# x's second half loaded a step later and normalised by VectorE, and 44 products of constants ahead of the first modulation product

## The chip, the cores and the metric

The kernel runs on one core of one Trainium2 chip. A core has TensorE (PE in the rows; its weight load is PEld), VectorE (DVE), ScalarE (ACT), GpSimd (POOL) and SyncE (SP), which here issues most DMA transfers. The metric is the device time of one execution in microseconds (us); less is better.

## The reference

One layer of a diffusion backbone: 1024 tokens x 1024 channels, 256 context tokens, all in float32. What matters here is its beginning:

```python
shift, scale, gate = jnp.split(jax.nn.silu(c) @ w_mod[i] + b_mod[i], 3, axis=-1)
mod_c = jax.nn.silu(c_ctx) @ w_mod[i] + b_mod[i]
h = _layer_norm(x) * (1.0 + scale[:, None]) + shift[:, None]
hc = _layer_norm(ctx) * (1.0 + mod_c[D_MODEL:2 * D_MODEL]) + mod_c[:D_MODEL]
discs = [_discretise(ssm_lam_re[i, k], ssm_lam_im[i, k], ssm_log_dt[i, k],
                     ssm_b_re[i, k], ssm_b_im[i, k]) for k in range(2)]
u_ctx = hc @ w_in[i][:, :D_SSM] + b_in[i][:D_SSM]
...
ua, za, ub, vb, zb, ga, gb = _split_proj(h @ w_in[i] + b_in[i])
y_a, _ = _s5_bidir(ua, discs, ssm_c_re[i], ssm_c_im[i], ssm_d[i], ctx_final, True)
```

Behind it come the two branches (the bidirectional S5 scan `y_a`, and a spatial gating unit), their gates, an output projection and a LayerNorm of the residual. `_discretise` turns the S5 parameters into the scan's coefficients, elementwise on arrays of 64 x 64.

## The kernel before

Every product in float32 precision is made of three products of rounded halves (`mm3`, lines L82, L83, L84: high x high, low x high, high x low). So each operand is split into a high part, which ScalarE writes (a rounding copy), and a low part, which VectorE subtracts (`split`, L77 and L78).

The stage of the change is the first 90 us. Its work goes over eight blocks k of 128 input channels, and over two halves of the tokens: half 0 is the tiles x0 to x3, half 1 is x4 to x7 (each 128 tokens x 1024 channels, 512 KB). Per block:

- `load_wm(k)` loads two blocks of w_mod of 512 KB; they take buffers of a pool of six, so those of k + 3 wait for the products of k. `load_uw` loads a raw chunk of the weight of `ua` (for two k) and splits it.
- `mod_mm(k)` makes the modulation product `pm` (8 products, 16 records), `mod(k)` copies it on VectorE (`mrow`), brings it into columns with products `pmc` on TensorE and adds the bias on VectorE (`mods`).
- `trans_pe(k, hf)` transposes block k of four tiles of x on TensorE (`pt`); `trans_mod` reads it on ScalarE with scale and shift (`hf`), rounds it on ScalarE (`hh`) and takes the low part on VectorE (`hl`).
- `ua_step(k, hf)` runs the 12 products `pu` of the block, into four PSUM banks that collect over k.

`norm_rows` is LayerNorm without its gain: statistics on VectorE, a power -0.5 on GpSimd, a small operation on VectorE, and the normalisation itself on ScalarE (L198). Only x3 is normalised by VectorE (L453). The first loop runs the eight steps of half 0 and prepares block k + 2 within step k; in steps 1 to 4 it also loads and normalises x4 to x7. The second loop runs half 1 and the context tiles (`trans_c`: `pc`, `ch`, `cl`). The discretisation stands as a list `later` of small VectorE operations (tiles `disc`, then `cmul` with its scratch `cmu` and `cmv`, and the results `pw` and `pb`); `issue(n)` puts the next n of them into the order: 8 in each step of half 0, 12 in each of half 1. When `pb` is there, VectorE and GpSimd make the products `ab`. Behind the second loop TensorE goes on with `pcu`, the context's input projection. `ua_out` reads the banks of a half on ScalarE (`ut`).

A scheduler of the framework sets the final order of each engine from the order in the code and from its own estimates; `tc.issue_after(i)` holds the instructions in it back until behind instruction i. Each engine, and SP's queue of loads, then works strictly in its order.

Much later, at 405 to 436 us, `y_mm(b)` makes the scan's output for four blocks b from tables that `y_tables(b)` loads: `ca` for two directions, then `mt`.

Of the kernel before, what the change touches and what calls it, by code (L numbers as in the profile page):

```python
# [12 lines left out]
OP = mybir.AluOpType  # L13
# [23 lines left out]
def mixer_kernel(ctx: ExitStack, tc: tile.TileContext, a, out):  # L37
    nc = tc.nc
    V, S, Pl, PE = nc.vector, nc.scalar, nc.gpsimd, nc.tensor
# [5 lines left out]
    def pool_of(tag, bufs, dshape, ddt=F32):  # L45
        def make(name, shape=dshape, dt=ddt):
            return sb.tile(list(shape), dt, name=name, tag=tag, bufs=bufs)
        return make
# [5 lines left out]
    TMP = pool_of("tmp", 4, (128, 512))  # L54
    ROW = pool_of("row", 2, (128, 1280))
    ST = pool_of("st", 12, (128, 12))

    def C(name, shape, dt=F32):
        return sb.tile(list(shape), dt, name=name)

    def BANK(name, shape=(128, 512)):
        return psum.tile(list(shape), F32, name=name, tag="b", bufs=8)

    def dma(o, i):
        nc.sync.dma_start(o, i)

    def dma_side(o, i):

# [23 lines left out]
    def emit_load():  # L92
        key, ap, shape, eng = jobs[emitted[0]]
        emitted[0] += 1
        raw = RAW("r_" + key, shape)
        dma(raw, ap)
        hi, lo = WSP("h_" + key, shape), WSP("l_" + key, shape)
        split(hi, lo, raw, eng)
        loaded[key] = (hi, lo)
# [29 lines left out]

    cc = C("cc", [128, 8, 2])  # L130
    dma(cc, a["cc"])
    wmt = {}

    def load_wm(k):
        for s in range(2):
            wmt[k, s] = WSP(f"wm{k}{s}", (128, 4, 256), F32)
            dma(wmt[k, s], a["wm"][k, s])

    xv = a["x"].rearrange("(t p) d -> t p d", p=128)
    xn = {}  # L140

    def load_x(t):
        xn[t] = G(f"x{t}")
        dma(xn[t], xv[t])
# [15 lines left out]
    ident = C("ident", [128, 128])  # L160
# [3 lines left out]
    ones = C("ones", [128, 128])  # L164
# [15 lines left out]
    def moments(src, name):  # L180

        n = src.shape[-1] // 512
        st = ST(name + "s")[:, :6 * n].rearrange("p (n s) -> p n s", n=n)
        for i in range(n):
            V.bn_stats(st[:, i, :], src[:, i * 512:(i + 1) * 512])
        return finish(st, name)

    def finish(st, name):
        mv = ST(name + "m")
        V.bn_aggr(mv[:, 0:2], st)  # L190
        V.tensor_scalar(mv[:, 2:3], mv[:, 1:2], EPS, None, op0=OP.add)
        Pl.tensor_tensor(mv[:, 3:4], mv[:, 2:3], half, op=OP.pow)
        return mv, mv[:, 0:1], mv[:, 3:4]

    def norm_rows(x, name):
        mv, mu, rs = moments(x, name)
        V.scalar_tensor_tensor(mv[:, 4:5], mu, -1.0, rs, op0=OP.mult, op1=OP.mult)
        S.activation(x, x, AF.Identity, bias=mv[:, 4:5], scale=rs)  # L198
# [21 lines left out]
    def mod(k):  # L220
        if k not in pms:
            mod_mm(k)
        pm = pms[k]
        row = TMP("mrow")
        V.tensor_copy(row[:, 0:256], pm[:, 0:256])
        pc = BANK(f"pmc{k}")
        for s in range(2):
            PE.matmul(pc[:, 2 * s:2 * s + 2], row[:, 128 * s:128 * s + 128], fold[:, 0:2], start=True, stop=True)
        V.tensor_tensor(mods[:, k], pc[:, 0:4].rearrange("p (s n) -> p s n", s=2),
                        cols[:, k:k + 9:8].unsqueeze(2).to_broadcast([128, 2, 2]), op=OP.add)  # L230
# [3 lines left out]
    def trans_pe(k, hf):  # L234
        if hth[k] is None:
            hth[k] = G(f"hh{k}", dt=F32R)
            htl[k] = G(f"hl{k}", dt=F32R)
        p = pts[k, hf] = BANK(f"pt{k}{hf}")
        for i in range(4):
            PE.transpose(p[:, i * 128:(i + 1) * 128], xn[4 * hf + i][:, k * 128:(k + 1) * 128], ident)  # L240

    def trans_mod(k, hf):
        sl = slice(hf * 512, hf * 512 + 512)
        modulate(hth[k][:, sl], htl[k][:, sl], pts[k, hf], k, 0)

    def trans_h(k, hf):
        trans_pe(k, hf)
        trans_mod(k, hf)
# [4 lines left out]
    def load_uw(q):  # L253
        raw = RAW(f"uw{q}", (128, 2, 512))
        dma(raw, a["w_ua"][q])
        split(uw[:, 0, q], uw[:, 1, q], raw, V)
# [10 lines left out]
    def ua_step(k, hf):  # L267
        sl = slice(hf * 512, hf * 512 + 512)
        for b in range(4):
            if k == 0:  # L270
                acc[b] = BANK(f"pu{b}{hf}")
            mm3(acc[b], *uwk(k, b), hth[k][:, sl], htl[k][:, sl], k == 0, k == 7)
# [5 lines left out]
    def ua_out(hf):  # L278
        for b in range(4):
            if hf == 0:  # L280
                ut.append(WSP(f"ut{b}", (128, T, 128), F32))
            S.activation(ut[b][:, :, 64 * hf:64 * hf + 64], acc[b].rearrange("p (c t) -> p t c", t=T),
                         AF.Identity, bias=cols[:, C_UA + b:C_UA + b + 1])
            if hf == 1:
                dma(ud[b].rearrange("t p c -> p t c")[:, :, 32:160], ut[b])
# [8 lines left out]
    def issue(n):  # L294
        for f in later[:n]:
            f()
        del later[:n]
# [13 lines left out]
    def cp(o, x, scale=1.0):  # L311
        later.append(lambda: S.activation(o, x, AF.Copy, scale=scale))
# [34 lines left out]
    q, w, z, sn, cs, odd, eve, sg = (r_[i] for i in range(3, 11))  # L347
# [57 lines left out]
    def cmul(dst, x, yr, yi):  # L405

        n, w = x.shape[1], x.shape[3]

        def f():
            u = TMP("cmu", (128, 256 // w, 2, w))[:, :n]  # L410
            v = TMP("cmv", (128, 256 // w, 2, w))[:, :n]
            for o, y in ((u, yr), (v, yi)):
                V.tensor_tensor(o, x, y.unsqueeze(1).unsqueeze(1).to_broadcast([128, n, 2, w]), op=OP.mult)
            V.tensor_tensor(dst[:, :, 0, :], u[:, :, 0, :], v[:, :, 1, :], op=OP.subtract)
            V.tensor_tensor(dst[:, :, 1, :], u[:, :, 1, :], v[:, :, 0, :], op=OP.add)
        later.append(f)

    n = 1
# [27 lines left out]
    pc = pwf  # L446
    cp(pc[:, :, :, 0:32], pw[:, :, :, 0:32])

    with tc.issue_after(folded.ins):
        for t in range(3):  # L450
            norm_rows(xn[t], f"lx{t}")
        _, mu, rs = moments(xn[3], "lx3")
        normed = V.tensor_scalar(xn[3], xn[3], mu, rs, op0=OP.subtract, op1=OP.mult)  # L453

    with tc.issue_after(mod_mm(0).ins):
        trans_pe(0, 0)
# [8 lines left out]
    for k in range(8):  # L465
        if k >= 6:
            trans_h(k - 6, 1)
        ua_step(k, 0)
        if k >= 1 and k < 5:
            load_x(k + 3)  # L470
            norm_rows(xn[k + 3], f"lx{k + 3}")
        if k + 2 < 8:
            load_wm(k + 2)
            if k in (0, 1, 3):
                load_uw((k + 3) // 2)
            trans_pe(k + 2, 0)
            mod(k + 2)
            trans_mod(k + 2, 0)
        issue(8)

    xc = []
    for j in range(2):
        t = RAW(f"xc{j}")
# [5 lines left out]
    def trans_c(k):  # L489
        p = BANK(f"pc{k}")  # L490
        for j in range(2):
            PE.transpose(p[:, j * 128:(j + 1) * 128], xc[j][:, k * 128:(k + 1) * 128], ident)
        modulate(cth[k // 4][:, k % 4, :], ctl[k // 4][:, k % 4, :], p[:, :256], k, 1)
    ua_out(0)
    for k in range(8):
        if k + 2 < 8:
            trans_h(k + 2, 1)
        ua_step(k, 1)
        trans_c(k)
        issue(12)  # L500
    ua_out(1)

    weights("blk0", 0)
# [16 lines left out]
    for b in range(4):  # L520
        p = BANK(f"pcu{b}")
# [126 lines left out]
    mtd = dram.tile([4, 128, 8, 128], F32, name="mtd")  # L648

    cad = dram.tile([4, 2, 128, 1024], F32, name="cad")  # L650
# [67 lines left out]
    for q in range(4):  # L718
        wh, wl = weights(f"vb{q}")
        for kk in range(8):  # L720
            ks = slice(128 * kk, 128 * kk + 128)
            for j in range(2):
                k = 2 * q + j
# [4 lines left out]
    for kk in range(8):  # L728
        if kk % 2 == 0:
            vpair = G(f"vt{kk}", (128, 2, 512))  # L730
        v = vpair[:, kk % 2, :]
# [15 lines left out]
    for cb in range(4):  # L747
        V.scalar_tensor_tensor(sgb[:, cb, :], prs[:, cb, :], cols[:, C_LB + cb:C_LB + cb + 1], sgb[:, cb, :],
                               op0=OP.mult, op1=OP.add)
# [49 lines left out]
            then(t, p, sl)  # L799


    cas, mts, ums, zs, gks, gt = {}, {}, {}, {}, {}, []

    def y_tables(b):
        for d in range(2):
            ca = WSP(f"ca{b}{d}", (128, 8, 8, 16), F32)
            dma(ca.rearrange("p g i h -> p (g i h)"), cad[b, d])
            cas[b, d] = ca
        mts[b] = RAW(f"mt{b}", (128, 8, 128))
        dma(mts[b], mtd[b])  # L810
        if b < 2:
            y_rows(b)

    def y_rows(b):
        src = ud[b].rearrange("t (h g) c -> (t h) g c", g=8)[:, :, 32:160]
        if b < 2:
            t = ROW(f"um{b}", (128, 8, 128))
            dma(t, src)
            ums[b] = [t[:, g, :] for g in range(8)]
        else:  # L820
            ts_ = [TMP(f"um{b}{h}", (128, 4, 128)) for h in range(2)]
            for h, t in enumerate(ts_):
                dma(t, src[:, 4 * h:4 * h + 4])
            ums[b] = [ts_[g // 4][:, g % 4, :] for g in range(8)]
# [273 lines left out]
    for i in range(0, 8, 2):  # L1098
# [15 lines left out]
        if i == 0:  # L1114

            for h in range(2):
                p = BANK(f"pga{h}")
# [72 lines left out]
    for t in range(4, 8):  # L1190
        w = 512 if t < 7 else 256
# [67 lines left out]
```

## Time and profile before

| | us |
|---|---|
| time, median of 3 runs | 728.3 (727.65 to 730.11) |
| the profiled execution | 724.48 |
| its span, first to last instruction | 722.7 |
| TensorE busy | 692.4 (96% of the span) |
| VectorE busy | 528.4 (73%) |
| ScalarE busy | 252.5 (35%) |
| GpSimd busy | 92.0 (13%) |

The mean granted clock of TensorE was 0.994. Busy times are sums over the whole span; the stage of the change has a profile of its own, which is read from waits and timelines. In a timeline row stand the start, the busy time, engine, line, operation, output<-inputs, shape and count, and in brackets the idle time ahead of it with what ended it.

### The profile page before, as it was taken

The page shows a single profiled execution, that of the slowest core. Times are in us where ns is not written, and L with a number is a line of the kernel's source. Part 1 is how long each engine was busy: PE and PEld are TensorE (multiplying, and loading weights), DVE is VectorE, ACT ScalarE, POOL GpSimd, SP SyncE. Part 2 cuts the span into 40 slices and gives each one's busy share as a digit, 9 for nine tenths or more (in the row PEclk, how much of TensorE's full clock was granted, in tenths as well). Part 3 has the DMA queues.
Part 4 walks back from the last instruction along what each step waited for, and adds up shares of the span by engine and source line. Part 5 has one row for each costly group of instructions (what it writes and reads, how often), then busy time and mean ns, then how long its engine had stood idle before and what let it go on. Part 6 is the DMA issues. An engine that isn't in the chain of part 4 may idle for free.

```text
span 722.7 us, 10220 instructions
## 1 busy us (share of the span) xinstructions
PE 692.4 (96%) x3876; PEld 573.8 (79%) x3876; DVE 528.4 (73%) x1148; ACT 252.5 (35%) x364; POOL 92.0 (13%) x145
## 2 busy tenths in 40 slices
PE   3989999999999999999999999999999999999993
PEld 1657798888888888888888898888888878888883
DVE  5586954469889485898989399736678669953993
ACT  4348737652013523211112366324353522310000
POOL 1000134006642100000000000001111000000220
PEclk9999999999999999999999999999999999999997
DMA  7950283624721321121213753234557951251421
GB/s 304 412 194 2 58 219 125 183 79 169 230 77 34 107 70 56 58 88 59 88 59 94 250 210 102 88 106 171 173 188 284 411 214 40 88 175 57 176 88 59
DMA packets 41394, 101.96 MB, mean 141 GB/s; under 512 B 8961, under 2 KB 17793, under 8 KB 41345
## 3 DMA queue, kind: packets, MB, share of 16 engines
q1 hardware_dynamic: 35072, 84.04, 33.6%
q0 software_dynamic: 6272, 17.28, 7.0%
q8 instruction: 30, 0.49, 0.3%
q14 instruction: 20, 0.16, 0.1%
HBM read 79.31 MB, written 24.08 MB: 143 GB/s over the span
## 4 chain that ended last, share of the span: by engine, by line
PE 90%; DVE 3%; DMA 2%; ACT 2%; issue 1%; SPq 0%; POOL 0%; DVEq 0%
PE pp L82 10%; PE pp L83 10%; PE pp L84 10%; PE po L1155 4%; PE po L1154 4%; PE po L1153 4%; PE pb L84 4%; PE pb L83 4%; PE pb L82 4%; PE pg L83 4%; PE pg L82 4%; PE pg L84 4%; PE pv L572 3%; PE pvb L725 2%; PE pvb L724 2%; PE pvb L726 2%
## 5 line engine op out<-in xcount | busy, mean ns | idle before, releaser
L82 PE MATMUL pp<-hh,h_blk 128*128 128x512 f32 x320 | 125.3, 392 | 0.0
L83 PE MATMUL pp<-hh,l_blk 128*128 128x512 f32 x320 | 124.6, 389 | 0.0
L84 PE MATMUL pp<-hl,h_blk 128*128 128x512 f32 x320 | 124.5, 389 | 0.0
L82 PEld LDWEIGHTS pp<-hh,h_blk 128*128 128x128 f32 x320 | 60.1, 188 | 13.2 <-ACT vst L574 0.5
L84 PEld LDWEIGHTS pp<-hl,h_blk 128*128 128x128 f32 x320 | 60.1, 188 | 12.5
L83 PEld LDWEIGHTS pp<-hh,l_blk 128*128 128x128 f32 x320 | 60.1, 188 | 12.2
L634 DVE TENSOR_TENSOR scm<-acat,vst 128x128 f32<-128x128 f32 x158 | 46.0, 291 | 9.8 <-ACT vst L574 5.0
L77 ACT ACTIVATE h_blk<-r_blk 128x1024 fp32r<-128x1024 f32 x20 | 21.4, 1070 | 54.6 <-PE pp L83 21.7
L638 DVE TENSOR_TENSOR vst<-vst,scs 128x64 f32<-128x64 f32 x158 | 35.3, 224 | 4.9
L637 DVE TENSOR_TENSOR scs<-scm 128x64 f32<-128x64 f32 x158 | 35.4, 224 | 4.6
L78 DVE TENSOR_TENSOR l_blk<-r_blk,h_blk 128x1024 fp32r<-128x1024 f32 x20 | 25.2, 1258 | 17.0 <-ACT h_blk L77 17.0
L1153 PE MATMUL po<-wobig,mh 128*128 128x512 f32 (+1 forms) x90 | 32.9, 365 | 0.0
L1154 PE MATMUL po<-wobig,mh 128*128 128x512 f32 (+1 forms) x90 | 32.9, 365 | 0.0
L1155 PE MATMUL po<-wobig,ml 128*128 128x512 f32 (+1 forms) x90 | 32.9, 365 | 0.0
L82 PE MATMUL pu<-hh,uw 128*128 128x512 f32 x64 | 26.8, 419 | 3.9 <-ACT hh L208 3.9
L1165 DVE TENSOR_TENSOR r<-po,xr 128x512 f32<-128x512 f32 (+1 forms) x18 | 11.0, 618 | 22.2 <-PE po L1155 22.2
L788 ACT ACTIVATE act<-pp,cols 128x512 f32<-128x512 f32 x16 | 10.8, 678 | 46.5 <-issue 19.0
L84 PE MATMUL pu<-hl,uw 128*128 128x512 f32 x64 | 25.2, 406 | 1.1 <-DVE hl L209 1.1
L69 POOL DMA_DIRECT2D md<-mb x8 | 4.3, 543 | 168.1 <-DVE scs L637 110.7
L82 PE MATMUL pb<-yas,h_w_a 128*128 128x512 f32 x64 | 25.3, 395 | 0.0
L83 PE MATMUL pu<-hh,uw 128*128 128x512 f32 x64 | 25.3, 395 | 0.0
L725 PE MATMUL pvb<-l_vb,hh 128*128 128x512 f32 x64 | 25.0, 391 | 0.0
(415 smaller groups left out, 1711.7 us busy)
## 6 DMA issues: line engine op xcount, KB each, us to landing
r_blk<-in_w_blk SPq DMA_DIRECT2D x20, 512.0 KB, 3.4
wm<-in_wm SPq DMA_DIRECT2D x16, 512.0 KB, 8.2
x<-in_x SPq DMA_DIRECT2D x8, 512.0 KB, 6.8
cad<-kca POOLq DMA_DIRECT2D x8, 512.0 KB, 3.3
md<-mb POOLq DMA_DIRECT2D x8, 512.0 KB, 3.2
ca<-cad SPq DMA_DIRECT2D x8, 512.0 KB, 5.6
ga<-in_w_blk SPq DMA_DIRECT2D x8, 512.0 KB, 3.7
wgt<-in_w_gate SPq DMA_DIRECT2D x8, 512.0 KB, 3.6
```

The costliest lines, as they stand in the source:

```text
L78: return first, (eng or V).tensor_tensor(lo, src, hi.bitcast(F32), op=OP.subtract)
L82: PE.matmul(o, wh, rh, start=first, stop=False, skip_group_check=more)
L83: PE.matmul(o, wl, rh, start=False, stop=False, skip_group_check=more)
L84: PE.matmul(o, wh, rl, start=False, stop=last, skip_group_check=more)
L572: PE.matmul(p[64 * par:64 * par + 64, c, 0:160], abt[:, 2 * q + par, 64 * c:64 * c + 64], u160[b][:, 2 * q + par, :], start=True, stop=True)
L634: V.tensor_tensor(scm, acat.rearrange("p d (o c) q -> p d o (c q)", o=2), both(n - 1, prev).unsqueeze(2).to_broadcast([128, 2, 2, 32]), op ...
L637: V.tensor_tensor(scs4, m4[:, :, 0, :], m4[:, :, 1, :], op=OP.add)
L638: V.tensor_tensor(both(n, 160 if n == 31 else cur), both(n, cur), scs2, op=OP.add)
L725: PE.matmul(pvb[kk], hth[k][:, ks], wl[:, j, :], start=False, stop=False)
L1153: PE.matmul(p, mh, wh, start=k == 0, stop=False)
L1154: PE.matmul(p, mh, wl, start=False, stop=False)
L1155: PE.matmul(p, ml, wh, start=False, stop=k == 7)
```

## The change

Four things, in the diff below. 44 products of two constant tiles (`ones`, `ident`) stand at the head of the program for TensorE, into a bank that nobody reads. x4 to x7 are loaded behind the w_mod blocks of steps 2, 3 and 4 (the last two together) and normalised one step after that by VectorE, in place (`norm_here`). The list `later` is issued 8 at a time up to step 4, then 4, and 14 in the second loop; the scratch of `cmul` lies in the ROW buffers. In `y_tables` the table mt of block 3 is loaded behind the two `ca` of block 2.

```diff
 def dma(o, i):
-        nc.sync.dma_start(o, i)
+        return nc.sync.dma_start(o, i)
...
+    def norm_here(t):
+        _, mu, rs = moments(xn[t], f"lx{t}")
+        return V.tensor_scalar(xn[t], xn[t], mu, rs, op0=OP.subtract, op1=OP.mult)
...
-            u = TMP("cmu", (128, 256 // w, 2, w))[:, :n]
-            v = TMP("cmv", (128, 256 // w, 2, w))[:, :n]
+            u, v = (ROW(t)[:, 0:512].rearrange("p (n c w) -> p n c w", c=2, w=w)[:, :n] for t in ("cmu", "cmv"))
...
+    warm = BANK("warm")
+    for i in range(44):
+        PE.matmul(warm[:, 0:128], ones, ident, start=True, stop=True)
     with tc.issue_after(folded.ins):
         for t in range(3):
             norm_rows(xn[t], f"lx{t}")
-        _, mu, rs = moments(xn[3], "lx3")
-        normed = V.tensor_scalar(xn[3], xn[3], mu, rs, op0=OP.subtract, op1=OP.mult)
+        normed = norm_here(3)
...
         ua_step(k, 0)
-        if k >= 1 and k < 5:
-            load_x(k + 3)
-            norm_rows(xn[k + 3], f"lx{k + 3}")
         if k + 2 < 8:
             load_wm(k + 2)
+
+            for t in {2: (4,), 3: (5,), 4: (6, 7)}.get(k, ()):
+                load_x(t)
             if k in (0, 1, 3):
                 load_uw((k + 3) // 2)
             trans_pe(k + 2, 0)
             mod(k + 2)
             trans_mod(k + 2, 0)
-        issue(8)
+        for t in {3: (4,), 4: (5,), 5: (6, 7)}.get(k, ()):
+            norm_here(t)
+        issue(8 if k < 5 else 4)
...
         trans_c(k)
-        issue(12)
+        issue(14)
...
-            dma(ca.rearrange("p g i h -> p (g i h)"), cad[b, d])
+            ca_last[b] = dma(ca.rearrange("p g i h -> p (g i h)"), cad[b, d])
...
-        dma(mts[b], mtd[b])
+        if b == 3:
+
+            with tc.issue_after(ca_last[2].ins):
+                dma(mts[b], mtd[b])
+        else:
+            dma(mts[b], mtd[b])
```

How that moves the instructions, at three places. First SP's queue of loads, from x4 on. In the order before x_277, x_342, x_403 and x_468 are x4 to x7, wm_353 and wm_355 the blocks of k = 4, wm_414 and wm_416 those of k = 5, wm_479 and wm_481 of k = 6, uw_418 the chunk uw3:

```order
L65 DMA x_277<-in_x 128x1024
L65 DMA wm_353<-in_wm 128x1024
L65 DMA wm_355<-in_wm 128x1024
L65 DMA wm_414<-in_wm 128x1024
L65 DMA x_342<-in_x 128x1024
L65 DMA wm_416<-in_wm 128x1024
L65 DMA uw_418<-in_w_ua 128x1024
L65 DMA x_403<-in_x 128x1024
L65 DMA wm_479<-in_wm 128x1024
L65 DMA wm_481<-in_wm 128x1024
```

And after, where the blocks of k = 4 are wm_376 and wm_378, those of k = 5 wm_428 and wm_430, of k = 6 wm_492 and wm_494, and x_380 is x4:

```order
L65 DMA wm_376<-in_wm 128x1024
L65 DMA wm_378<-in_wm 128x1024
L65 DMA wm_428<-in_wm 128x1024
L65 DMA wm_430<-in_wm 128x1024
L65 DMA uw_434<-in_w_ua 128x1024
L65 DMA x_380<-in_x 128x1024
L65 DMA wm_492<-in_wm 128x1024
L65 DMA wm_494<-in_wm 128x1024
L65 DMA x_432<-in_x 128x1024
```

x4 now goes behind five loads that it stood ahead of; the loads in front of this place stand as they did.

Second, ScalarE from the split of uw0 on. Before (hh_160 is of k = 0, hh_179 of k = 1, hh_231 of k = 2, hh_296 of k = 3, hh_357 of k = 4; uw_227, uw_292 and uw_418 are the chunks uw1, uw2 and uw3):

```order
L77 ACTIVATE uw<-uw_79 128x512 x2
L207 ACTIVATE hf<-pt_162,mods 128x512
L208 ACTIVATE hh_160<-hf 128x512
L207 ACTIVATE hf<-pt_181,mods 128x512
L208 ACTIVATE hh_179<-hf 128x512
L77 ACTIVATE uw<-uw_227 128x1024
...
L198 ACTIVATE x_277<-x_277,lx4m 128x1024
L207 ACTIVATE hf<-pt_359,mods 128x512
L208 ACTIVATE hh_357<-hf 128x512
L198 ACTIVATE x_342<-x_342,lx5m 128x1024
L77 ACTIVATE uw<-uw_418 128x1024
L207 ACTIVATE hf<-pt_424,mods 128x512
```

After (hh_205 is of k = 0, hh_224 of k = 1, hh_276 of k = 2, hh_330 of k = 3; uw_272, uw_326 and uw_434 are uw1, uw2 and uw3):

```order
L77 ACTIVATE uw<-uw_79 128x512 x2
L211 ACTIVATE hf<-pt_207,mods 128x512
L212 ACTIVATE hh_205<-hf 128x512
L77 ACTIVATE uw<-uw_272 128x1024
L211 ACTIVATE hf<-pt_226,mods 128x512
L212 ACTIVATE hh_224<-hf 128x512
L77 ACTIVATE uw<-uw_326 128x1024
L211 ACTIVATE hf<-pt_278,mods 128x512
L212 ACTIVATE hh_276<-hf 128x512
L211 ACTIVATE hf<-pt_332,mods 128x512
L212 ACTIVATE hh_330<-hf 128x512
L77 ACTIVATE uw<-uw_434 128x1024
```

The normalisations of x4 to x7 are gone from this engine, and the split of uw1 has moved ahead of `hf` of k = 1.

Third, VectorE at the end of the second half. Before (hl_534 is the last `hl`, that of k = 7; cl_650 belongs to the context, ab_1089 is the first of the products `ab`):

```order
L413 TENSOR_TENSOR cmu<-pw,disc 128x448
L414 TENSOR_TENSOR pb<-cmu,cmv 128x7x32
L415 TENSOR_TENSOR pb<-cmu,cmv 128x7x32
L413 TENSOR_TENSOR cmv<-pw,disc 128x448
L414 TENSOR_TENSOR pb<-cmu,cmv 128x7x32
L415 TENSOR_TENSOR pb<-cmu,cmv 128x7x32
L209 TENSOR_TENSOR hl_534<-hf,hh_533 128x512
L209 TENSOR_TENSOR cl_650<-hf,ch_648 128x256
L538 TENSOR_TENSOR ab_1089<-pb,xb 128x1024
```

After (the last `hl` is hl_559):

```order
L417 TENSOR_TENSOR pb<-cmu,cmv 128x7x32
L418 TENSOR_TENSOR pb<-cmu,cmv 128x7x32
L416 TENSOR_TENSOR cmu<-pw,disc 128x448
L416 TENSOR_TENSOR cmv<-pw,disc 128x448
L213 TENSOR_TENSOR hl_559<-hf,hh_558 128x512
L417 TENSOR_TENSOR pb<-cmu,cmv 128x7x32
L418 TENSOR_TENSOR pb<-cmu,cmv 128x7x32
L213 TENSOR_TENSOR cl_679<-hf,ch_677 128x256
L546 TENSOR_TENSOR ab_1130<-pb,xb 128x1024
```

The last `hl` stands two products `pb` further ahead. Not shown: between the context's first `lc0m` and this place VectorE's order holds 29 more small operations of the discretisation than before, and fewer ahead of it.

## Rows read from the trace of the kernel before

**Rows 1.** The page's chain that ended last: shares of the span by engine.
```profile
PE 90%; DVE 3%; DMA 2%; ACT 2%; issue 1%; SPq 0%; POOL 0%; DVEq 0%
```

**Rows 2.** Waits of TensorE: who waited <- for whom: us, times, longest us.
```profile
PE pm L217 <- DMA wm<-in_wm: 10.9, 1, 10.9
PE pu L82 <- ACT hh L208: 3.9, 3, 2.2
PE pu L84 <- DVE hl L209: 1.1, 2, 0.9
PE py L848 <- DMA ca<-cad: 0.8, 1, 0.8
```

**Rows 3.** Timeline of TensorE, 16 to 27 us.
```profile
16.31 1.94 PE L217 MATMUL pm<-wm,sc 128*32 128x256 f32 x16
...
22.12 0.60 PE L240 MATMUL pt<-ident,x 128*128 128x128 f32 x4
22.64 1.07 PE L217 MATMUL pm<-wm,sc 128*32 128x256 f32 x16
23.64 0.50 PE L82 MATMUL pu<-hh,uw 128*128 128x512 f32 x1
...
26.99 0.60 PE L240 MATMUL pt<-ident,x 128*128 128x128 f32 x4
```

**Rows 4.** Timeline of TensorE at 420 us: eight records of 128x128.
```profile
419.55 1.04 PE L858 MATMUL pg<-ident,gk 128*128 128x128 f32 x8
420.42 0.39 PE L846 MATMUL py<-mt,um 128*128 128x128 f32 x2
```

**Rows 5.** Timeline of ScalarE, 19 to 66 us.
```profile
19.64 0.78 ACT L207 ACTIVATE hf<-pt,mods 128x512 f32<-128x512 f32 x1 [1.99 <-DVE mods L229]
20.45 0.63 ACT L208 ACTIVATE hh<-hf 128x512 fp32r<-128x512 f32 x1
21.38 1.06 ACT L77 ACTIVATE uw<-uw 128x1024 fp32r<-128x1024 f32 x1 [0.30 <-DMA uw<-in_w_ua]
...
43.29 1.25 ACT L198 ACTIVATE x<-x,lx5m 128x1024 f32<-128x1024 f32 x1 [3.35 <-DVE lx5m L197]
...
64.18 2.42 ACT L282 ACTIVATE ut<-pu,cols 128x512 f32<-128x512 f32 x4
```

**Rows 6.** Timeline of TensorE: `pu` of k = 5, half 1's first, and `pcu`.
```profile
46.86 0.51 PE L82 MATMUL pu<-hh,uw 128*128 128x512 f32 x1 [2.15 <-ACT hh L208]
...
62.56 0.39 PE L82 MATMUL pu<-hh,uw 128*128 128x512 f32 x1
...
89.95 0.28 PE L82 MATMUL pcu<-ch,uw 128*128 128x256 f32 x1
```

**Rows 7.** Busy times in two stretches: PE, PEld, DVE, ACT, POOL, PEclk, DMA share, GB/s.
```profile
20.00:40.00 20.00, 19.02 (x131) 12.14 (x129) 12.76 (x49) 8.53 (x11) 0.55 (x1) 1.00 1.03 410
60.90:87.05 26.15, 25.98 (x132) 21.12 (x130) 20.45 (x61) 22.20 (x53) 2.74 (x2) 1.00 0.18 41
```

**Rows 8.** Timelines of VectorE and GpSimd.
```profile
14.84 0.80 DVE L453 TENSOR_SCALAR x<-x,lx3m 128x1024 f32<-128x1024 f32 x1
...
27.96 0.48 DVE L309 SCALAR_TENSOR_TENSOR disc<-disc 128x64 f32<-128x64 f32 x2
...
29.89 0.35 DVE L306 TENSOR_TENSOR disc<-disc 128x64 f32<-128x64 f32 x2
...
83.63 0.38 DVE L415 TENSOR_TENSOR pb<-cmu,cmv 128x224 f32<-128x224 f32 x1
...
84.89 2.23 DVE L415 TENSOR_TENSOR pb<-cmu,cmv 128x224 f32<-128x224 f32 x1
87.05 0.68 DVE L209 TENSOR_TENSOR hl<-hf,hh 128x512 fp32r<-128x512 f32 x1
...
84.68 2.19 POOL L538 TENSOR_TENSOR ab<-pb,xb 128x1024 f32<-128x1024 f32 x1 [22.57 <-DVE cmv L413]
```

**Rows 9.** Timeline of VectorE at 424 us.
```profile
424.24 4.16 DVE L837 COPY z<-vst 64x512 f32<-64x512 f32 x6
```

More of the change, by code (lines that the diff above doesn't have):

```diff
@@ L799, in branch @@
             then(t, p, sl)
-    cas, mts, ums, zs, gks, gt = {}, {}, {}, {}, {}, []
+    ca_last, cas, mts, ums, zs, gks, gt = {}, {}, {}, {}, {}, {}, []
     def y_tables(b):
```

## The prediction

> **What bounds the kernel now.** I read the chain first, then the waits of TensorE, then the places of the waits in the timelines. TensorE carries 90% of the chain [rows 1]; so an edit on another engine is worth what it takes off TensorE's idle time, and a product added to TensorE costs its own duration unless TensorE would have idled there. The list of waits [rows 2] names where that idle time is: 10.9 us before the first modulation product, 3.9 us in three waits of `pu` for ScalarE's `hh`, 1.1 us in two waits of `pu` for VectorE's `hl`, 0.8 us of `py` for a table `ca`; nothing else on the list is above 0.5 us. All but the `py` wait stand ahead of 90 us, and from there TensorE has no wait of more than a few tenths till 420 us. A gain that is still there when `pcu` starts (89.95 [rows 6]) therefore reaches the end of the kernel nearly whole. The question is what the change moves that one start.
>
> The longest `hh` wait shows what kind they are: ScalarE has the normalisation of x5 ahead of the `hf` that TensorE needs, 1.25 us at 43.29, then the split of uw3, and TensorE waits 2.15 us until 46.86 [rows 5, 6]. The wait at x7 is alike; the third and shortest, at x4, follows VectorE, which has x4's statistics ahead of the modulation. The engines have the time; their order is what is late. The DMA engines are full from 20 to 40 us (share 1.03, 410 GB/s [rows 7]), but no `pm` behind the first is on the list of waits, so transfers don't gate this stage directly.
>
> **The change, part by part.**
>
> *The 44 products.* They stand at the head of TensorE's order and use only constants, so they fall into the 10.9 us in which it idles. A float32 product leaves two records: 88. At full clock a record of this shape takes 0.109 us (eight in the 0.87 us from 419.55 to the next row at 420.42 [rows 4]), hence 88 x 0.109 = 9.6 us; at the lower level of 1.2 GHz instead of 2.4 it is double, 19.2 us. That the clock is low at the start is read from durations, since the granted-clock column has no record there and prints 1.00: sixteen `pm` records take 1.94 us at 16.31 and 1.07 us at 22.64 [rows 3]. Between these the clock rose, at most some 8 us after the first product at 10.89. With constants ready at about 1.5 us and the clock rising X us after the first warm product, they end at 11.1 + 0.5 X: 11.1 for X = 0, 15.1 for X = 8. I take X = 5: 13.6. So they probably outlast the landing of the first wm block by up to 2 or 3 us, but `pm0` and what follows then run at twice the speed they had (1.07 for 1.94 us), and the modulation's first `mrow` has to stand behind the split of uw0 on VectorE anyway, which now comes first there. Net: the first `pu` about where it was or some tenths earlier. The Trainium skill, page "TensorE: Matmul & The Clock Gate", Part 1, says that the low clock is the default and sustained work releases it, for which it recommends such products; by that rule X is short and they end nearer 11 than 15; the sum would be the same, because the next wait hides it.
>
> That next wait is at k = 1. ScalarE's order now has the split of uw1 ahead of `hf` of k = 1; before it stood behind. The split started at 21.38, released by uw1's landing, and that landing can't come earlier, since the queue ahead of it is unchanged and full. 21.38 + 1.06 (split) + 0.78 + 0.63 (`hf`, `hh` [rows 5]) = 23.85, for a `pu` that started at 23.64 [rows 3]. **Term 1: +0.2 us.** Whatever the head gains, this swallows; it costs nothing more as long as the warm products end by about 14.8.
>
> *x normalised by VectorE.* x4 to x7 leave ScalarE (four times 1.24) and go to VectorE at 0.80 each, as x3 did before [rows 8]; one small operation each goes. All three `hh` waits lose their cause: 3.9 us. The later place of x in the queue of loads also lets wm and uw land ahead, and puts x's statistics behind the next `hl`: the `hl` wait of this half, 0.2 (1.1 less the 0.9 at 87 us), goes too. With `pm` no longer cut in halves between the `pu` products the steps come close to an undisturbed one, 22.12 to 26.99 = 4.87 us [rows 3]; walking the eight steps so gives 58.05 for the first `pu` of the second half, where ScalarE's three read-outs `ut` (0.6 each, four in 2.42 [rows 5]) and two `hf` hold it. Before it was 62.56 [rows 6]. **Term 2: -4.7 us; together -4.5 at the half.** If only the listed waits go it is -3.9.
>
> *Discretisation issued later (8, then 4, then 14 a step).* This pays VectorE for the normalisations: 29 more small operations are left for the second half. They are not free there. From 60.90 to 87.05 VectorE was busy 20.45 of 26.15 us [rows 7] and the last `hl` came late at 87.05, behind a `pb` product of 2.23 us, and TensorE waited. After: 20.45, less the two `pb` now behind that `hl` (2.23 + 0.38 = 2.6 [rows 8]), plus an `hl` now inside (0.6), plus 29 small ones at 0.18 = 5.2 (two take 0.35 in one row and 0.48 in another [rows 8]; I take the first): 23.65. Starting at 58.3, 2.6 earlier than before, the last `hl` begins at 81.95 and ends at 82.6, if VectorE never waits. The 2.23 us is no normal price: the same line costs 0.38, and Pool's product `ab` of 2.19 us lay over it [rows 8]. The Pool product starts when the first `pb` half is there, so in the new order it meets an operation just ahead of the last `hl`: +1.84, 84.4. The Trainium skill, page "SBUF — State Buffer", "SBUF: two separate sides", has the rule: VectorE and GpSimd share a port pair that one holds for a whole instruction. The trace agrees (2.23 beside 2.19); by that rule the stall follows Pool's product to its new place, without it the sum would be 1.8 us better. I keep the block in the sum, because the row repeats nowhere without Pool. From the last `hl` to `pcu` it was 89.95 - 87.73 = 2.2; so 86.6, and 0.4 for the context's last `ch`/`cl` behind the `ut` on ScalarE: 87.0. **Term 3: +1.6 given back; -2.9 at 90 us.**
>
> *Scratch of `cmul` in the two ROW buffers*: the other users of these are done before or come later in the order. I cost it at nothing; wrong, it is a wait of some tenths on VectorE, within the spread of term 3.
>
> *mt3 behind the two `ca`.* Both tables land one transfer of 512 KB sooner, 1.28 us at the 410 GB/s above. `py` waited 0.8 for `ca` [rows 2]. But VectorE's copies `z`, 4.16 us to 428.4 [rows 9], gate the last `py` stage soon behind it. Between 0 and 1.3 I take 0.4. **Term 4: -0.4.**
>
> Sum: +0.2 - 4.7 + 1.6 - 0.4 = -3.3. The profiled execution was 724.48 us, so 721.2; the same off the median of 728.3 is 725.0.
>
> **The rivals.** *No give-back.* If VectorE has room in the second half (the small ones go into its idle time and Pool blocks nothing ahead of the last `hl`), TensorE alone sets the end: -4.5 at the half and -0.9 for the `hl` wait, then the 0.4: -5.8, 722.5. For it speaks that VectorE idled 5.7 us there; against it, that most of these lay early in the half, in a wait for ScalarE, and that the Pool stall is seen. *VectorE becomes the bound.* With the small ones at 0.24 (7.0 us), 25.4 + 1.84 from 58.3 ends the last `hl` at 86.2 and `pcu` starts at 88.8: -1.1, with the rest -1.5: 726.8, no measurable change. For it: VectorE is the only engine that gets work, and each small one that stands behind another's result pays its whole length. *The other side: warm products that stay slow.* If the clock doesn't rise under these products, they last 19.2 us and end at 20.7. From an end of 14.8 each microsecond moves k = 1 by as much: +5.9, net +2.6, 730.9; the change is slower than before from an end of 18.1 on. Against it: in the trace the clock rose under products and transposes with gaps between them.
>
> **How the numbers follow.** My forecast, give-back of a part, has 0.44, and lies between 723.5 and 726.1. No give-back 0.22. VectorE as the bound 0.27. Slow warm products 0.07. Faster by over 0.3% (2.2 us, about what a measurement of this kernel tells from none) are the first two: 0.66; the third is within it: 0.27; the last is slower: 0.07. The range leaves out the last case and the tails of both neighbours: 721.8 to 728.3.
>
> **What would show it.** Right: `warm` ends between 11 and 15 us and `pm0` takes about 1.0 us; the first `pu` of k = 1 starts near 23.85, that of the second half near 58; no wait of `pu` for `hh` over 0.5 us between 35 and 62 us; the last `hl` ends near 84.4 with a long VectorE operation beside Pool's `ab` ahead of it; `pcu` starts near 87.0; the `py` wait for `ca` is gone and about 0.4 us of it kept. Wrong: `pcu` at 85 or earlier (VectorE had room), at 88.5 or later with `pu` waiting for `hl` at several k (VectorE bound), `pm0` behind 18 us (clock), or a wait of `hl` or `mods` at k = 3 to 5 behind the new normalisations on VectorE, which I hold at some tenths.

## The result and the profile after

The changed kernel takes 721.4 us (median of 5 executions, 718.94 to 722.85), the kernel before 728.43 (median of 5, 727.65 to 730.37). The ratio is 0.9893, 95% interval 0.9864 to 0.9921: faster by 7.0 us or 1.07%. The forecast was 725.0, in 721.8 to 728.3: the sign was right, the size half of what came, and the time lies 0.4 us below the range.

One thing must be known to read this. Executions of one and the same kernel here differ by more than the effect of most edits, and the mean granted clock of TensorE goes with a part of it. Of 95 executions of the kernel before that were timed in the course of this study, the 24 at a clock of 0.995 have a median of 724.8 us, the 20 at 0.991 one of 727.6, the 13 at 0.989 one of 730.1; the median of all is 727.5, the least 723.8. The clock does not tell the whole: the 35 at 0.993 and 0.994 have medians of 728.1 and 727.1, as slow as those at 0.991. The mean leaves out the start of the program, where the clock column has no record and reads 1.00 while records run at half speed [rows 3]. Of the 95 only 7 are quicker than the profiled execution that the prediction was worked from (724.48). Of the changed kernel the execution behind the profile below is the median one (721.4, clock 0.991); its two quickest, at 0.994 and 0.995, took 719.1 and 718.9.

The waits of TensorE in the changed kernel (who waited <- for whom: us, times, longest us), against [rows 2]:

```profile
PE pu L82 <- ACT hh L212: 3.3, 2, 2.0
PE warm L455 <- POOL ident masks.py:199: 1.5, 1, 1.5
PE pg L871 <- ACT gk L863: 1.0, 1, 1.0
PE py L861 <- DMA ca<-cad: 0.9, 1, 0.9
```

The 10.9 us for the first wm block have gone and so have the waits for `hl`. But `hh` is still there, in two other places. TensorE's timeline shows where, against [rows 3] and [rows 6]:

```profile
1.50 12.62 PE L455 MATMUL warm<-ident,ones 128*128 128x128 f32 x88 [1.50 <-POOL ident masks.py:199]
14.05 1.07 PE L221 MATMUL pm<-wm,sc 128*32 128x256 f32 x16
...
25.25 0.50 PE L82 MATMUL pu<-hh,uw 128*128 128x512 f32 x1 [2.02 <-ACT hh L212]
...
27.34 0.63 PE L84 MATMUL pu<-hl,uw 128*128 128x512 f32 x1
27.77 0.63 PE L82 MATMUL pu<-hh,uw 128*128 128x512 f32 x1
28.19 0.63 PE L83 MATMUL pu<-hh,uw 128*128 128x512 f32 x1
...
30.32 0.80 PE L244 MATMUL pt<-ident,x 128*128 128x128 f32 x4
...
60.32 0.50 PE L82 MATMUL pu<-hh,uw 128*128 128x512 f32 x1 [1.29 <-ACT hh L212]
...
86.41 0.36 PE L82 MATMUL pcu<-ch,uw 128*128 128x256 f32 x1
```

The products end at 14.05 and the first `pm` runs at full clock. The `pu` of k = 1 waits 2.02 us. Two microseconds later consecutive `pu` stand 0.43 us apart instead of 0.23: the clock has fallen from 2.4 to 1.2 GHz, until about 31 us. From the first `pu` of k = 1 to the next `pt` it is 5.07 us (25.25 to 30.32), where the kernel before took 3.35 (23.64 to 26.99 [rows 3]): 1.7 us are lost by it. The windows of this kernel (busy times as in [rows 7]; the third number from the right is the granted clock) say the same, 0.87 and 0.96:

```profile
20.00:30.00 10.00, 7.98 (x44) 5.55 (x43) 4.55 (x8) 4.71 (x6) 0.00 (x0) 0.87 1.03 412
30.00:40.00 10.00, 10.00 (x73) 7.18 (x72) 6.68 (x30) 3.77 (x5) 0.00 (x0) 0.96 0.87 318
```

What made `hh` of k = 1 late is on ScalarE, where the split of uw1 started 1.4 us later than in [rows 5], again released by its landing:

```profile
22.81 1.06 ACT L77 ACTIVATE uw<-uw 128x1024 fp32r<-128x1024 f32 x1 [4.86 <-DMA uw<-in_w_ua]
23.77 0.76 ACT L211 ACTIVATE hf<-pt,mods 128x512 f32<-128x512 f32 x1
24.56 0.63 ACT L212 ACTIVATE hh<-hf 128x512 fp32r<-128x512 f32 x1
```

[rows 5] shows an early landing there: in a second profile of the kernel before, whose order is the same, that split started at 22.21 us:

```profile
22.21 1.06 ACT L77 ACTIVATE uw<-uw 128x1024 fp32r<-128x1024 f32 x1 [0.78 <-DMA uw<-in_w_ua]
```

And the end of the second half on VectorE and GpSimd, against [rows 8]:

```profile
82.47 0.68 DVE L213 TENSOR_TENSOR hl<-hf,hh 128x512 fp32r<-128x512 f32 x1
83.07 0.38 DVE L417 TENSOR_TENSOR pb<-cmu,cmv 128x224 f32<-128x224 f32 x1
...
85.30 2.10 DVE L213 TENSOR_TENSOR cl<-hf,ch 128x256 fp32r<-128x256 f32 x1
...
84.44 2.68 POOL L546 TENSOR_TENSOR ab<-pb,xb 128x1024 f32<-128x1024 f32 x1 [21.57 <-ACT pwf L316]
```

The last `hl` is done at 83.15, in time: no `pu` waits. The operation that Pool's product stretches is now a `cl` (2.10 us, 0.42 otherwise), which `pcu` needs late. VectorE's part of this half, from the end of a pair of `hl` to the start of the last `hl`, was 26.15 us with 20.45 busy in [rows 7]; in the changed kernel it is

```profile
61.51:82.47 20.96, 20.96 (x110) 17.42 (x109) 19.74 (x85) 18.08 (x45) 0.62 (x1) 1.00 0.17 43
```

85 operations in place of 61, in 0.7 us less of busy time, with 1.2 us idle in place of 5.7.

So the balance of the two profiled executions is: k = 1 starts 1.6 us later (25.25 for 23.64); the first `pu` of the second half 2.2 earlier (60.32 for 62.56), with the 1.7 us of low clock in it; `pcu` 3.5 earlier (86.41 for 89.95); the span ends 3.1 earlier (719.6 for 722.7).

### The profile page after: what moved, and what is told of

Its sections match the earlier page's. It is cut to its first block, busy times and chain, and to the rows that moved or that the text cites. A ratio compares the mean times of both kernels' runs of the same rounds, so it can differ in the third digit from the quotient of the medians.

```text
span 719.6 us, 10385 instructions
## 1 busy us (share of the span) xinstructions
PE 700.4 (97%) x3964; PEld 587.3 (82%) x3964; DVE 529.4 (74%) x1148; ACT 248.8 (35%) x360; POOL 92.6 (13%) x145
## 4 chain that ended last, share of the span: by engine, by line
PE 87%; DVE 5%; DMA 3%; ACT 3%; issue 1%; SPq 0%; POOL 0%; DVEq 0%; ACTq 0%
PE pp L82 10%; PE pp L83 10%; PE pp L84 10%; PE po L1168 4%; PE po L1167 4%; PE po L1166 4%; PE pb L84 4%; PE pb L83 4%; PE pb L82 4%; PE pg L82 4%; PE pg L83 4%; PE pg L84 4%; PE pv L580 3%; DMA uw<-in_w_ua 3%; PE pvb L732 2%; PE pvb L733 2%
## 5 line engine op out<-in xcount | busy, mean ns | idle before, releaser
L796 ACT ACTIVATE act<-pp,cols 128x512 f32<-128x512 f32 x16 | 10.9, 678 | 46.5 <-issue 19.0
```

## The experiments

Two questions are open from this. Why did the median fall by 7.0 us when the two profiles differ by 3.1? And which part of the change did it?

**The kernel before, again.** No edit.

> The kernel before, unchanged, to see what its own executions differ by. Theory A (clock): its profiled execution at 724.5 us was one without a low stretch of TensorE's clock behind its waits, and most timed ones have such a stretch; then the runs near 728 to 730 us list a mean granted clock under 0.992, and a run near 724.5 lists 0.994 or more; a profile of a slow one shows pu products at double spacing somewhere in 18 to 62 us. Rival B (spread elsewhere): the granted clock is 0.994 in all runs, and the 4 us lie outside the first 90 us.

Measured: 728.64 us (12 executions, 724.68 to 730.89), ratio 1.002 (0.9995 to 1.0044). The clock goes with the time: 0.989 in six executions from 729.5 to 730.9, 0.991 in three at 727.3 to 727.8, 0.994 in the three quickest. Its profile was again a quick one. For these 12, theory A holds as far as the clock goes. Over all 95 it holds only for the longest: 16 of the 17 executions above 729 us list 0.991 or less, but 21 of the 49 at 727.5 or more list 0.993 or 0.994. No execution of this kernel itself near 730 us was profiled; where low stretches lie shows in the trace of the last experiment below, which has the same order up to 400 us and another only in the loads behind.

**Only the products, and only the rest.** The kernel before with the 44 products, and the changed kernel without them:

```diff
+    warm = BANK("warm")
+    for i in range(44):
+        PE.matmul(warm[:, 0:128], ones, ident, start=True, stop=True)
```

> The kernel before with only the 44 products added. Theory A: the three hh waits stay and uw1's split moves ahead of hf of k = 1 here too, so the time is 726 to 729 us, no measurable change. Rival C (the products are what the gain comes from, because pm, pt and the first pu run at full clock): 721 to 723 us.

Measured: 720.45 us, ratio 0.9921 (0.9892 to 0.9949). Theory A's 726 to 729 is refuted: the products alone bring 0.8%. The waits of this kernel show what I had not thought of:

```profile
PE pmc L228 <- DVE mrow L225: 1.6, 2, 1.0
PE warm L451 <- POOL ident masks.py:199: 1.5, 1, 1.5
PE pu L82 <- ACT hh L208: 1.3, 2, 0.7
PE pu L84 <- DVE hl L209: 0.9, 1, 0.9
```

Nothing was done about x here, and yet the 3.9 us for `hh` of [rows 2] are 1.3. The framework's scheduler takes the products for 88 records of TensorE time, comes to other estimates for all that follows, and orders ScalarE, VectorE and TensorE anew. The half gets as short as in the changed kernel: from the first `pu` of k = 1 to that of the second half it is 33.54 us, where the kernel before took 38.92 (23.64 to 62.56 [rows 3, 6]), with x4 to x7 still on ScalarE and no later than before (x5 at 40.12 for 43.29 [rows 5]). TensorE's rows stand first, then ScalarE's:

```profile
24.42 0.50 PE L82 MATMUL pu<-hh,uw 128*128 128x512 f32 x1 [0.61 <-ACT hh L208]
...
57.96 0.48 PE L82 MATMUL pu<-hh,uw 128*128 128x512 f32 x1
...
36.12 1.24 ACT L198 ACTIVATE x<-x,lx4m 128x1024 f32<-128x1024 f32 x1 [3.48 <-DVE lx4m L197]
40.12 1.24 ACT L198 ACTIVATE x<-x,lx5m 128x1024 f32<-128x1024 f32 x1 [0.48 <-DVE lx5m L197]
```

> The changed kernel without the 44 products; ScalarE's order then has hf of k = 1 ahead of uw1 again. Theory A: the hh waits of k = 4 to 7 are gone and with them the places where the clock falls: 718.5 to 721.5 us, no worse than the changed kernel. Rival C: 725 to 727 us.

Measured: 724.38 us (12 executions, 722.5 to 725.83), ratio 0.9954 (0.9935 to 0.9973): worse than the changed kernel, so theory A's 718.5 to 721.5 falls here too, and rival C's 725 to 727 is missed by 0.6. The loads, the normalisation, the list and mt's place bring 0.5% of their own, about the size that I had forecast for all. On top of the products they are not shown to bring anything: 0.9893 (0.9864 to 0.9921) for the whole change and 0.9921 (0.9892 to 0.9949) for the products alone overlap.

**uw1's split behind k = 1.** The changed kernel with the splits of uw1 and uw2 behind `hh` of k = 1 and 2:

```diff
+        if q in (1, 2):
+            with tc.issue_after(rounded[q, 0].ins):
+                split(uw[:, 0, q], uw[:, 1, q], raw, V)
+        else:
+            split(uw[:, 0, q], uw[:, 1, q], raw, V)
```

> The changed kernel with the splits of uw1 and uw2 behind hh of k = 1 and k = 2, as before the change. Theory A: the 2.0 us wait at k = 1 goes (to under 0.5 us), and with it the low stretch of the clock behind it: 717 to 719 us, spread under 1.5 us, pcu at 82.5 to 84. Rival B (the wait costs only its length beyond what the second half gives back): 720 to 721.4 us.

Measured: 719.82 us (718.47 to 721.9), ratio 0.9898 (0.987 to 0.9926): the interval lies nearly where that of the changed kernel does, so as a time it is undecided. The median falls between the two forecasts, and the spread is 3.4 us, not under 1.5. In the trace the wait is gone and no low stretch follows; TensorE's timeline:

```profile
23.60 0.50 PE L82 MATMUL pu<-hh,uw 128*128 128x512 f32 x1
...
57.76 0.50 PE L82 MATMUL pu<-hh,uw 128*128 128x512 f32 x1 [1.28 <-ACT hh L213]
...
83.84 0.36 PE L82 MATMUL pcu<-ch,uw 128*128 128x256 f32 x1
```

`pcu` is 6.1 us earlier than in [rows 6]. This profiled execution still took 721.9 us: behind a wait of `py` for `ca` (1.89 us at 424.57) the clock was low again for some 3 us.

**Products without the reordering.** With 16 products the order of all engines is that without any, save four rows that moved past each other. So these two change what TensorE does at the head, and nothing else: `range(44)` becomes `range(16)`, in the kernel before and in the changed one.

> The kernel before with 16 products instead of 44. With 16 the order of all engines stays that of the kernel before (four rows differ), with 44 the framework's scheduler orders ScalarE and VectorE otherwise. Theory O (order): the 44 products gain by that reordering, so here 726 to 729 us, the hh waits of 3.9 us as before. Theory H (hardware: TensorE's clock is up before the first pm): 720 to 722 us as with 44.

Measured: 726.69 us, ratio 0.9996 (0.9975 to 1.0017); the waits of [rows 2] for `hh` and `hl` stand there to the tenth. Theory O's range; but the trace shows that H was not tested yet (windows):

```profile
8.00:11.00 3.00, 0.00 (x0) 0.00 (x0) 2.15 (x8) 1.68 (x2) 0.55 (x1) 1.00 1.01 407
11.00:13.00 2.00, 1.27 (x12) 0.42 (x16) 1.29 (x6) 1.69 (x2) 1.08 (x2) 0.54 1.04 424
```

The products ended at 6.7 us, TensorE idled for 5.0 until the first block landed, and the granted clock was 0.54 when `pm` ran.

> The changed kernel with 16 products; its order is that of the changed kernel without any (four rows differ), hf of k = 1 ahead of uw1. Theory O: 723 to 725 us, as without products (724.4). Theory H: 719.5 to 721.5 us.

Measured: 721.75 us, ratio 0.9927 (0.9906 to 0.9948), against 0.9954 (0.9935 to 0.9973) without products: better by a point estimate of 2 us, with intervals that overlap. It lies between O's 723 to 725 and H's 719.5 to 721.5, and H is not tested here either: the products ended at 7.9 us, TensorE idled, and the first `pm` ran at half speed. It does show the half without the reordering: 37.2 us from k = 1 to the second half.

```profile
11.22 2.26 PE L221 MATMUL pm<-wm,sc 128*32 128x256 f32 x16 [3.36 <-DMA wm<-in_wm]
...
22.98 0.50 PE L82 MATMUL pu<-hh,uw 128*128 128x512 f32 x1
...
60.17 0.39 PE L82 MATMUL pu<-hh,uw 128*128 128x512 f32 x1
```

**Products up to the first block.** 30 narrow products first, then 14 of the full width, so that TensorE stays busy while the scheduler, which prices columns, leaves its order:

```diff
-    for i in range(44):
-        PE.matmul(warm[:, 0:128], ones, ident, start=True, stop=True)
+    for i in range(44):
+        w = 128 if i >= 30 else 2
+        PE.matmul(warm[:, 0:w], ones, ident[:, 0:w], start=True, stop=True)
```

> The kernel before with 30 products of 2 columns and then 14 of 128 columns ahead of the first pm; the order of all engines stays that of the kernel before (four rows differ). With 16 products TensorE stood idle for 5 us behind them and the granted clock was down again (0.54 from 11 to 13 us); here they reach to about 13 us. Theory H (the clock at the head is a cost of its own): no execution loses the 3 us of a late rise, so 724 to 725.5 us, least runs 723.5 to 724, none above 728.5. Theory O alone (order): 727 to 728.5 us with the spread of the kernel before.

Measured: 733.19 us, ratio 1.0087 (1.0056 to 1.0119). My price for narrow products was wrong; they took as long as wide ones at the low clock, 0.21 us a record, and the 88 records end at 20.4 (TensorE's timeline):

```profile
1.50 18.98 PE L452 MATMUL warm<-ident,ones 128*128 128x2 f32 x88 [1.50 <-POOL ident masks.py:199]
20.42 1.07 PE L217 MATMUL pm<-wm,sc 128*32 128x256 f32 x16
```

So it tells nothing on H, but it is the rival of the other side made real: products that end at 20.4 us make the kernel slower, by 0.9%.

> The changed kernel with the same 30 narrow and 14 wide products; its order is that of the changed kernel without products (hf of k = 1 ahead of uw1), so the 2.0 us wait at k = 1 doesn't arise. H and O together: 718.5 to 720.5 us, better than the changed kernel by 1 to 2 us, least run near 718. O alone: 723 to 724.5 us, as without products.

Measured: 730.58 us, ratio 1.0041 (1.002 to 1.0062), by the same accident: `pm` at 19.93.

With 13 narrow and 14 wide ones they end in time. `range(44)` is `range(27)` there and the wide ones begin at 13:

> The kernel before with 13 products of 2 columns and then 14 of 128: at 0.213 us a record, as the narrow ones took in the run with 30 of them, they end near 13 us, right ahead of the first pm; the order of all engines stays that of the kernel before (six rows differ). H: executions no longer lose the late rise at the head: median 724 to 725.5 us, none at 730. O: median 727 to 728.5 us with the same spread as the kernel before.

Measured: 725.8 us (722.73 to 726.37), ratio 0.9964 (0.9948 to 0.9981). `pm` stands at 12.62 and runs at full clock, none of 12 executions is above 726.4, the least is 1 us below the least of the 95; the `hh` waits are 3.9 us as before. The median misses H's range by 0.3 us and O's by 1.2. The head's clock is a gain by itself, of 0.36%; as the 44 products alone bring 0.8%, the order has a part, too. It could be more: in this profile the clock was low again from 19 to 22 us (0.75 in the window 19 to 25), behind the 1.5 us wait for `mrow`.

> The changed kernel with the same 13 narrow and 14 wide products, in its order without products. If head clock and order both count: 719 to 721 us, against 724.4 without products and 721.4 for the changed kernel. If the gain of the 44 products is their reordering alone: 723 to 725 us.

Measured: 722.58 us (719.89 to 724.35), ratio 0.9918 (0.9894 to 0.9941), between the two forecasts; 0.36% below the ratio without products (0.9954), with intervals that overlap, as in the pair with 16. In the new order the gain of the head's clock is thus a point estimate and not shown.

**Another count.** The kernel before with 32 products gets a third order.

> The kernel before with 32 products: they end near 11.5 us, about where the first wm block lands, and the scheduler's order is a third one, neither that of before nor that with 44. H: full clock at the head as with 44, hence no 730 us runs. O: the time follows the sum of hh, hl and mrow waits that this order has; if that is near the 2.2 us of the order with 44, 720 to 722 us, if near the 5.0 us of before, 724 to 725 us.

Measured: 727.62 us, ratio 1.0001 (0.9977 to 1.0025), no gain. H's signs came, the first `pm` at full clock and no run above 728.8, but no gain with them. What this order has is (waits, and a window)

```profile
PE pmc L228 <- DVE mrow L225: 3.1, 4, 2.0
PE pu L82 <- ACT hh L208: 3.0, 2, 2.5
...
19.00:25.00 6.00, 5.85 (x19) 4.80 (x20) 2.78 (x5) 2.46 (x3) 0.00 (x0) 0.58 1.03 416
```

TensorE waited 2.0 us for `mrow` until 15.9 us and had a clock of 0.58 from 19 to 25. The sum of the waits is near 7 us, more than either of O's two cases. With 44 products the same edit gives 0.8%, with 32 nothing: a full clock at the first `pm` is not enough, and what the order gives is no smooth function of the count.

**The engine that normalises.** The changed kernel with x4 to x7 on ScalarE: `norm_here(t)` becomes `norm_rows(xn[t], f"lx{t}")` in the loop.

> The changed kernel with x4 to x7 normalised by ScalarE again (their later loads and all else stay); the scheduler's order has them on ScalarE behind hf of k = 5 and later. My forecast's reason (ScalarE's normalisations ahead of hf are the cause of the waits): some hh waits return and 1 to 4 us are lost, 722 to 725 us. Rival (the order is what matters, not the engine): 720 to 722 us, as the changed kernel.

Measured: 720.28 us (718.69 to 724.42), ratio 0.9913 (0.9885 to 0.9941): the rival's range. Its profile is without a low stretch (span 717.3, clock 0.995), and it waits for `hh` and `hl` no more than the changed kernel does:

```profile
PE pu L82 <- ACT hh L212: 2.0, 2, 1.3
PE warm L455 <- POOL ident masks.py:199: 1.5, 1, 1.5
PE pmc L232 <- DVE mrow L229: 1.4, 2, 0.9
...
PE pu L84 <- DVE hl L213: 0.3, 1, 0.3
```

In this kernel ScalarE normalises x4 at 42.2 us, between an `hf` and its `hh`, and x5 at 46.4, ahead of an `hf` as before the change; the half takes 33.6 us all the same (24.77 to 58.39). So it was not the other engine that freed TensorE. Nor does it take the later place: the kernel with the products alone has the short half with x4 to x7 earlier.

**mt and ca.** The changed kernel without that edit, and the kernel before with it alone.

> The changed kernel with mt of block 3 loaded ahead of the two ca of block 2, as before the change; nothing else differs in the order. By my forecast 0.4 us longer, by the lag in the traces (nothing gained between 405 and 436 us) the same within 0.3: 719 to 723 us. A run at a mean granted clock of 0.994 or more shows the first 90 us without a low stretch: pcu near 84 us then, if the low stretch at 27 to 31 us of the changed kernel's profile cost 2.3 us.

Measured: 720.23 us (718.72 to 721.23), ratio 0.9903 (0.9881 to 0.9925), not to be told from the time with the edit. Its profile too has a low stretch behind the wait at k = 1 (26 to 30 us).

> The kernel before with only the order of mt and ca changed. My forecast: py waits for ca shrink by 1.3 us and 0.4 us is left at 436 us. Rival: nothing is left, since the blocks' other copies gate the same place.

Measured: 730.52 us, one execution, clock 0.989. From `pcu` to the first `pp` behind `py` it is 345.60 us here (96.64 to 442.24) for 346.24 in the kernel before (89.95 to 436.19), 0.64 less. But the kernel before with 27 products, without this edit, has 345.69 (91.94 to 437.63), so the gain is not shown. In the changed kernel the stretch is 346.71, without the edit 346.46: nothing gained there. The use of this run is another: its profile is of an execution of the old order at 730 us, and shows where 6 us go. All of them lie ahead of `pcu`, which starts 6.7 us later than in [rows 6]:

```profile
20.60 0.77 PE L82 MATMUL pu<-hh,uw 128*128 128x512 f32 x1
21.18 0.63 PE L83 MATMUL pu<-hh,uw 128*128 128x512 f32 x1
21.60 0.63 PE L84 MATMUL pu<-hl,uw 128*128 128x512 f32 x1
...
27.80 0.50 PE L82 MATMUL pu<-hh,uw 128*128 128x512 f32 x1
...
50.00:60.00 10.00, 9.02 (x45) 5.03 (x46) 6.78 (x32) 3.56 (x5) 0.55 (x1) 0.66 0.17 54
```

The first three rows are the timeline at k = 0: `pu` 0.43 us apart, the clock not yet up, so that k = 1 starts at 27.80 for 23.64 in [rows 3]. Of these 4.2 us 0.9 are no clock: the first wm block landed later (first `pm` at 11.83 for 10.89). The last row is the window behind the 2.2 us wait for `hh` at k = 5, at 0.66; ten microseconds at this clock lose 3.4 (an estimate, for a busy TensorE).

## Why the prediction was wrong

**The last step of the sum failed most: "the same off the median".** I took the difference of 3.3 us from a profile at 724.48 and subtracted it from a median of 728.3, as if the 3.8 us between them were a constant of both kernels. They are not. Off the profiled execution the sum gives 721.2, and the changed kernel's profiled execution, which is also its median, took 721.4: the miss of 3.6 us is this step. Quickest against quickest the kernels differ by 4.9 us (723.8, the least of the 95, and 718.9), median against the median of the 95 by 6.1, against the five executions of the result by 7.0; so 0.9 of the 7.0 is that those five lie above that median. Part of what the longer executions of the kernel before lose, and its profiled one did not, is stretches at 1.2 GHz, at the head and behind the longest wait: the execution at 730.5 us, in the old order, shows both. How many executions have which is not shown, since of the others only the mean clock is known. That the head's clock is worth something by itself is shown in the old order (0.36%), not in the new.

**"Whatever the head gains, this swallows"** (term 1) was wrong in two ways. The products did end where I said (14.05 for 13.6), and k = 1 did wait behind uw1; but uw1 landed 1.4 us later than in the trace of before, which shows an early landing, so the term was +1.6 and not +0.2, and behind the wait of 2.02 us came a low clock that cost 1.7 more. And the products were not worth nothing: alone they make 0.8%, in good part by another order of the other engines. I had read the order of the changed kernel as a consequence of the edits to x; that the products alone turn it was to be seen from the orders before any run.

**Term 2, -4.7,** came near its size and not for its reason, which was "All three `hh` waits lose their cause" with x on VectorE. Where k = 1 doesn't wait, the half takes 34.2 us from its first `pu` of k = 1 to that of the second half (23.60 to 57.76), as I had walked it (23.85 to 58.05); in the changed kernel's own profile it is 35.1 with the low clock in it. But with x back on ScalarE it is 33.6, and with the products alone, x on ScalarE and in its old place in the code, 33.5. With the edits to x and no reordering (16 products) it is 37.2, of 38.9 before. What shortened the half is the order that the 44 products bring; by this profile the edits to x and the list alone gave 1.7 us of it.

**Term 3, +1.6 given back, fell.** The second half took 26.1 us (60.32 to 86.41) for 27.4, 1.3 less. My 23.65 us of VectorE's time were 19.74, and so it kept up, although it started its part at 61.51 where I had 58.3: 29 more small operations and all, the last `hl` ended at 83.15, between my 82.6 and 84.4. The Pool product did not start where I had it, with the first `pb` half, but at 84.44, released by a `pwf`, behind the last `hl`. Its stall went to a `cl` that nobody waited for. The rule of the Trainium skill ("SBUF — State Buffer", "SBUF: two separate sides") still fits, 2.10 us beside 2.68; my place for it was wrong. The rival "no give-back" (722.5, chance 0.22) was the right one of the three for this half.

**Term 4, -0.4:** not shown in the old order, nothing in the new.

Term by term the two profiles give +1.6 (for +0.2), -3.9 (for -4.7, the low clock in it), -1.3 (for +1.6) and +0.5 (for -0.4). These errors cancel; that the profiles differ by 3.1 us, close to my 3.3, is luck. The rival on the other side, products that end too late, was sound: at 20.4 us the kernel was slower by 0.9%, where I had 0.36%.

What stays open: how the 0.8% of the products alone divide between order and clock beyond the point estimates (0.4% by clock alone, the rest order), since intervals are half a per cent wide; what the executions at 0.993 and 0.994 lose; and why a wait of 2.2 us in the old order brought a low clock in two profiles of that order and none in four. No version clearly beats the changed kernel: 719.8 (uw1 and uw2 later), 720.2 (without mt's edit), 720.3 (x on ScalarE) and 720.5 (products alone) have ratios within its interval.

## What to carry to other kernels

Before a difference of profiles is put on a median, look where the profiled execution stands among the timed ones; if it is one of the quickest, ask what the others have that it hasn't, and whether the change touches that. Where a framework orders the instructions by its own estimates, an added instruction that costs nothing can reorder everything behind it: undo the reordering (here by a count that left the order alone) before a gain is credited to what the instruction does. And when a part of a change is argued to be the cause, run the change without that part: the engine that normalises x looked like the heart of it and made no difference that could be measured.

## What the runs showed of the hardware

TensorE's clock fell behind short waits in the middle of dense work: after 2.02 us without an instruction, `pu` ran at half speed from 27 to 31 us. The same is seen behind 1.5 us (changed kernel without products, from 46.5 us), 1.89 us (`py`, at 425 us) and 2.0 us (32 products); in other executions waits of that length left it up (2.15 us at k = 5 in the kernel before). Such a stretch cost 1.7 us in the changed kernel, near the length of the wait itself, and by the granted clock about 3.4 us in the execution of the old order at 730.5 us (0.66 over 10 us, an estimate). The Trainium skill, "TensorE: Matmul & The Clock Gate", "HAM oscillation — how this bites in real kernels", tells of the same loss behind waits for DMA that are longer; here it comes behind shorter ones, on other engines too.

Products of 2 columns cost 0.21 us a record at the head, as much as those of 128 columns at the low clock, and the clock did not rise under them: 88 records, 60 of them narrow, took 18.98 us, and from 15 to 20 us, where all are wide, 25 stood in 5 us. In the changed kernel 55 records of that width stood in the 6 us from 8 to 14.
